# Hybrid decoder trunk on one core: the low halves of streamed weights and blocks formed by GpSimd instead of VectorE

## The chip, the core and the metric

The kernel runs on one core of a Trainium2 chip. The core has five engines with an instruction queue each: TensorE (PE, with its weight loads shown apart as PEld), VectorE (DVE), ScalarE (ACT), GpSimd (POOL) and SyncE (SP, which here only issues DMAs). An engine works through its queue in order and waits on semaphores. The metric is the time on the device in microseconds; the median of three runs before the change is 1358.11 us (1356.87 to 1358.42).

## What is computed

A decoder trunk of two layers over one sequence of 1024 positions with 1024 features, float32 in and out. Cut to what matters:

```python
def even_mixer(h, w_in, ...):                      # layer 0
    xa, ga, q, k, v, gb = split(h @ w_in)          # one projection, six parts
    ya = rg_lru(conv(xa)) * silu(ga)
    q, k = rms_norm(q, q_g), rms_norm(k, k_g)      # per head of 128
    yb = stick_breaking_attention(q, k, v) * silu(gb)
    return concatenate([ya, yb]) @ w_out

def odd_mixer(h, w_in, ...):                       # layer 1
    u, g = split(h @ w_in)
    y = gelu(s5_ssm(u))
    y = y * sigmoid(y @ glu_w + glu_b)
    return (y * silu(g)) @ w_out

for layer in range(2):
    h, gate = ada_modulate(x, c, ...)              # norm, scale, shift from c
    x = x + gate * mixer(h)
```

## The kernel before

Float32 products are made from two halves each: an operand x is split into a high half hi (x rounded to the fp32r format) and a low half lo = x - hi, and a product is hi*hi + hi*lo + lo*hi, three matmuls. Activations are split once and kept; weights are streamed from HBM and split as they come. The method `split` does it for a tensor that lies in SBUF: ACT casts to hi, DVE subtracts to lo (lines 72 and 75). The method `load_split` takes one of the two buffers of the pool `raw` (128 x 1024 floats), has SP load into it, and splits it.

Three things go through `load_split`:
- the weights of all projections (`w_raw`, `w_hi`, `w_lo`), 60 pieces of 128 x 1024: `w_fetch` keeps one piece ahead, with two buffers each for hi and lo. They serve the eight attention gates, the RG-LRU projections, the output projection of layer 0 (twice eight), the input projection of layer 1 (sixteen) and the GLU (eight).
- the q, k and v weights of heads 1 to 7 (`wqkv`), three chunks each, into a buffer that exists once, so that a chunk can be cast only when the last query block of the head before has been projected.
- the eight blocks of attention output (`yb`), written to HBM by the heads and loaded again for the output projection.

The two raw buffers are also used by the rows of the adaLN matrix (`ada_raw`), which DVE multiplies and sums in the heads (line 288, four rows a head), so all these loads stand in one line on SP, and each waits until the buffer two loads back is free.

The stages in order: a head part (norm of layer 0, to about 90 us), eight attention heads of about 67 us each (to 607), RG-LRU (to 790), the output projection in two halves (to 960), layer 1 with its S5 state space (to 1180), the GLU (to 1270) and the last projection. Within a head PE's order is written by hand: the gate's first matmuls, the transposes of the last query block's q and k (line 793), the rest of the gate, scores (lines 814 to 816), and then in turn qkv projections of eight query blocks for the next head (lines 767 to 769), transposes of the attention weights (line 832) and their products with v (lines 843 to 845). For each query block ACT squares q and k with a running sum (line 773), POOL turns the two sums into a factor (`pow_rstd`, lines 312 and 313), and DVE scales with it (line 776). The keep factors go through a scan on DVE (line 820), beta follows (lines 821, 822), PE transposes beta, and DVE forms the low half of the result (line 835).

POOL also issues the DMAs that write intermediate results to HBM: the tables of S5 (lines 689, 722, 729), the heads' output (962), the rotation tables (1215) that DVE makes in the output projection, x (1179), and in layer 1 the S5 inputs and outputs and the gates (1297, 1380, 1306). The order on DVE, ACT, POOL and SP is set by a scheduler that estimates when each instruction could run; only PE's order is the program's.

Of the kernel before, what the change touches and what calls it, by code (L numbers as in the profile page):

```python
# [9 lines left out]
F32 = mybir.dt.float32  # L10
# [4 lines left out]
ALU = mybir.AluOpType  # L15
# [39 lines left out]
class Trunk:  # L55
# [10 lines left out]
        return self.tc.alloc_tile_pool(name=name, bufs=bufs, side=side, reuse_waits="tile", **kw)  # L66


    def split(self, raw, hi, lo, hi_engine="act"):
        nc = self.nc  # L70
        if hi_engine == "act":
            nc.scalar.copy(hi, raw)  # L72
        else:
            nc.vector.tensor_copy(hi, raw)
        nc.vector.tensor_sub(lo, raw, hi.bitcast(F32))  # L75

    def load_split(self, src, hi, lo):
        raw = self.rp.tile([P, 1024], F32, name="w_raw", tag="raw")
        self.nc.sync.dma_start(raw, src)
        self.split(raw, hi, lo)  # L80
        return raw

    def w_next(self, ahead=1):
# [1548 lines left out]
```

## Time and profile before

| | before |
|---|---|
| median of three runs | 1358.11 us |
| the profiled execution, its own time | 1358.47 us |
| its span | 1356.7 us |
| TensorE busy | 1319.6 us |
| VectorE busy | 1058.5 us |
| ScalarE busy | 639.0 us |
| GpSimd busy | 148.8 us |
| mean granted clock of TensorE | 0.999 of full speed |

A busy PE is not always PE at its peak, since matmuls overlap: one of 512 columns shows 0.39 us, and they start 0.23 us apart. The span is what lies between the first and the last record; the time of the execution has some 2 us more around it. The chain that ended last is followed back from the last instruction, at each step to what released it.

### The profile page before, as it was taken

Reading aid. Unit: us, or ns where it says so; the run is one execution under the profiler, and the core shown is the slowest. Engines: PE = TensorE matmul, PEld = TensorE weight load, DVE = VectorE, ACT = ScalarE, POOL = GpSimd, SP = SyncE. Lnnn points to the kernel's source line nnn. Section 1 sums busy time; section 2 is a strip of 40 time slices with the busy share of each in tenths; the row PEclk is TensorE's granted clock in tenths of the full one; section 3 lists DMA queues with packets and bytes.
Section 4 is the critical chain, followed back from the end, with each engine's and each line's share of the span. In section 5 each row is a group of like instructions: output and inputs, shape, how many; then the busy total and the mean of one; then the engine's idle time right before and its main releaser. Section 6 shows DMA issues by size and latency. Waiting matters only on the chain.

```text
span 1356.7 us, 18988 instructions
## 1 busy us (share of the span) xinstructions
PE 1319.6 (97%) x7020; PEld 1136.4 (84%) x7020; DVE 1058.5 (78%) x2049; ACT 639.0 (47%) x1270; POOL 148.8 (11%) x239
## 2 busy tenths in 40 slices
PE   7999999999999999999999999999999999999998
PEld 3898889999989898888887878888888888888777
DVE  7949988878787878988899787866588669754784
ACT  6544454545454545354998722123364434633421
POOL 0012212222212121210000000000000000000000
PEclk9999999999999999999999999999999999999999
DMA  8442051413141314312211164332448789454331
GB/s 321 164 145 78 28 174 49 128 50 128 50 128 50 128 50 129 111 59 76 68 40 55 47 237 151 109 125 98 150 156 256 224 236 256 121 170 135 93 124 62
DMA packets 73212, 168.16 MB, mean 124 GB/s; under 512 B 9536, under 2 KB 35264, under 8 KB 73120
## 3 DMA queue, kind: packets, MB, share of 16 engines
q1 hardware_dynamic: 62112, 128.34, 30.9%
q0 software_dynamic: 11008, 38.62, 7.9%
q8 instruction: 55, 0.90, 0.3%
q14 instruction: 37, 0.30, 0.1%
HBM read 126.10 MB, written 40.83 MB: 123 GB/s over the span
## 4 chain that ended last, share of the span: by engine, by line
PE 60%; DVE 25%; ACT 5%; DMA 3%; issue 3%; POOL 2%; DVEq 0%; ACTq 0%; POOLq 0%
PE bank L120 6%; PE bank L123 6%; PE bank L122 6%; PE bank L125 6%; PE bank L121 6%; PE bank L124 5%; DVE keep L820 3%; PE bank L767 3%; PE bank L769 3%; PE bank L768 3%; DMA ada_raw<-ada 3%; DVE ada_raw L288 2%; PE bank L832 1%; DVE wt_lo L835 1%; DVE beta L822 1%
## 5 line engine op out<-in xcount | busy, mean ns | idle before, releaser
L767 PE MATMUL bank<-wqkv_hi,h_hi 128*128 128x384 f32 x512 | 173.6, 339 | 0.0
L769 PE MATMUL bank<-wqkv_hi,h_lo 128*128 128x384 f32 x512 | 172.4, 337 | 0.0
L768 PE MATMUL bank<-wqkv_lo,h_hi 128*128 128x384 f32 x512 | 172.4, 337 | 0.0
L72 ACT CAST w_hi<-w_raw 128x1024 fp32r<-128x1024 f32 x60 | 63.0, 1049 | 198.7 <-PE bank L123 142.2
L75 DVE TENSOR_TENSOR w_lo<-w_raw,w_hi 128x1024 fp32r<-128x1024 f32 x60 | 73.1, 1218 | 36.3 <-ACT w_hi L72 36.1
L768 PEld LDWEIGHTS bank<-wqkv_lo,h_hi 128*128 128x128 f32 x512 | 96.6, 189 | 0.4
L767 PEld LDWEIGHTS bank<-wqkv_hi,h_hi 128*128 128x128 f32 x512 | 96.6, 189 | 0.3
L769 PEld LDWEIGHTS bank<-wqkv_hi,h_lo 128*128 128x128 f32 x512 | 96.5, 189 | 0.0
L120 PE MATMUL bank<-h_hi,w_hi 128*128 128x512 f32 x224 | 89.3, 399 | 0.0
L122 PE MATMUL bank<-h_hi,w_hi 128*128 128x512 f32 x224 | 87.8, 392 | 0.7 <-DVE xc L1009 0.7
L776 DVE TENSOR_SCALAR nat<-bank,ss 128x128 f32<-128x128 f32 x128 | 39.1, 345 | 62.7 <-POOL ss L313 46.3
L124 PE MATMUL bank<-h_hi,w_lo 128*128 128x512 f32 x224 | 87.3, 390 | 0.4 <-DVE w_lo L75 0.4
L123 PE MATMUL bank<-h_lo,w_hi 128*128 128x512 f32 x224 | 87.7, 391 | 0.0
L125 PE MATMUL bank<-h_hi,w_lo 128*128 128x512 f32 x224 | 87.7, 391 | 0.0
L121 PE MATMUL bank<-h_lo,w_hi 128*128 128x512 f32 x224 | 87.3, 390 | 0.0
L820 DVE TENSOR_TENSOR_SCAN keep<-keep,after 128x1024 f32<-128x1024 f32 (+3 forms) x64 | 86.4, 1349 | 0.0
L312 POOL TENSOR_SCALAR ss<-ss 128x2 f32<-128x2 f32 x64 | 36.1, 564 | 306.9 <-ACT nat L773 306.3
L778 ACT COPY nat<-bank 128x128 f32<-128x128 f32 x64 | 17.0, 266 | 96.4 <-DVE nat L776 96.4
L773 ACT ACTIVATE nat<-bank 128x128 f32<-128x128 f32 x128 | 34.3, 276 | 58.6 <-PE bank L769 40.0
L817 ACT ACTIVATE keep<-bank 128x512 f32<-128x512 f32 (+2 forms) x96 | 48.5, 505 | 20.3 <-PE bank L816 18.8
L832 PE MATMUL bank<-ident,beta 128*128 128x128 f32 x288 | 43.5, 279 | 12.1 <-DVE wt_lo L835 8.9
L288 DVE SCALAR_TENSOR_TENSOR ada_raw<-ada_raw,cs 128x1024 f32<-128x1024 f32 x39 | 47.6, 1220 | 9.0 <-DMA ada_raw<-ada 8.9
(434 smaller groups left out, 3724.2 us busy)
## 6 DMA issues: line engine op xcount, KB each, us to landing
ada_raw<-ada SPq DMA_DIRECT2D x39, 512.0 KB, 4.2
w_raw<-wqkv SPq DMA_DIRECT2D x21, 512.0 KB, 3.6
w_raw<-wfm SPq DMA_DIRECT2D x20, 512.0 KB, 3.6
w_raw<-woe SPq DMA_DIRECT2D x16, 512.0 KB, 3.7
w_raw<-wod SPq DMA_DIRECT2D x16, 512.0 KB, 4.2
x<-xT SPq DMA_DIRECT2D x8, 512.0 KB, 7.1
cx_s<-ce POOLq DMA_DIRECT2D x16, 256.0 KB, 2.8
win_s<-wsb POOLq DMA_DIRECT2D x16, 256.0 KB, 3.3
```

What stands on the lines that cost most here:

```text
L75: nc.vector.tensor_sub(lo, raw, hi.bitcast(F32))
L120: nc.tensor.matmul(ps[0], wh[:, k, :], rh[k][:, h0], start=first, stop=False)
L121: nc.tensor.matmul(ps[0], wh[:, k, :], rl[k][:, h0], start=False, stop=False)
L122: nc.tensor.matmul(ps[1], wh[:, k, :], rh[k][:, h1], start=first, stop=False)
L123: nc.tensor.matmul(ps[1], wh[:, k, :], rl[k][:, h1], start=False, stop=False)
L124: nc.tensor.matmul(ps[0], wl[:, k, :], rh[k][:, h0], start=False, stop=last)
L125: nc.tensor.matmul(ps[1], wl[:, k, :], rh[k][:, h1], start=False, stop=last)
L288: v.scalar_tensor_tensor(raw, raw, 1.0, self.cs, op0=ALU.mult, op1=ALU.mult, accum_out=m)
L767: nc.tensor.matmul(ps[:, 0:384], hh[:, k, ts], wqh[:, ks], start=(k == 0), stop=False)
L768: nc.tensor.matmul(ps[:, 0:384], hh[:, k, ts], wql[:, ks], start=False, stop=False)
L769: nc.tensor.matmul(ps[:, 0:384], hl[:, k, ts], wqh[:, ks], start=False, stop=(k == KT - 1))
L820: v.tensor_tensor_scan(rev, rev, self.after[:, T - n:T][:, ::-1], 1.0, op0=ALU.mult, op1=ALU.max)
```

## The change

`load_split` no longer calls `split`: ACT casts to hi as before, and the subtraction is issued on GpSimd, as a `tensor_tensor` with the same operands. `split` loses a parameter that nobody used, and goes on subtracting on VectorE for everything that is split in place (activations, conv outputs, gates, y). Two lines fewer stand ahead of all other code, so a line of the changed kernel has a number lower by two from there on.

```diff
-    def split(self, raw, hi, lo, hi_engine="act"):
+    def split(self, raw, hi, lo):
+        self.nc.scalar.copy(hi, raw)
+        self.nc.vector.tensor_sub(lo, raw, hi.bitcast(F32))
+
+    def load_split(self, src, hi, lo):
         nc = self.nc
-        if hi_engine == "act":
-            nc.scalar.copy(hi, raw)
-        else:
-            nc.vector.tensor_copy(hi, raw)
-        nc.vector.tensor_sub(lo, raw, hi.bitcast(F32))
-
-    def load_split(self, src, hi, lo):
         raw = self.rp.tile([P, 1024], F32, name="w_raw", tag="raw")
-        self.nc.sync.dma_start(raw, src)
-        self.split(raw, hi, lo)
+        nc.sync.dma_start(raw, src)
+        nc.scalar.copy(hi, raw)
+        nc.gpsimd.tensor_tensor(lo, raw, hi.bitcast(F32), op=ALU.subtract)
         return raw
```

The scheduler places the moved instruction anew. On POOL at the end of a head (here the second), before the change:

```order
L312 TENSOR_SCALAR ss<-ss 128x2
L313 TENSOR_TENSOR ss<-ss,mh 128x2
L722 DMA win_s_1132<-wsb 128x512
L729 DMA rp_s_1148<-rpad 128x240
L962 DMA yb_s_607<-yb 128x1024
L689 DMA cx_s_1141<-ce 128x4x128
```

and now (lines 310, 311, 720, 727, 960 and 687 are 312, 313, 722, 729, 962 and 689 of before; line 78 is the moved subtraction):

```order
L78 TENSOR_TENSOR wqkv_lo<-w_raw,wqkv_hi 128x1024 x2
L310 TENSOR_SCALAR ss<-ss 128x2
L311 TENSOR_TENSOR ss<-ss,mh 128x2
L720 DMA win_s_1132<-wsb 128x512
L727 DMA rp_s_1148<-rpad 128x240
L960 DMA yb_s_607<-yb 128x1024
L78 TENSOR_TENSOR wqkv_lo<-w_raw,wqkv_hi 128x1024
L687 DMA cx_s_1141<-ce 128x4x128
L78 TENSOR_TENSOR w_lo<-w_raw,w_hi 128x1024
```

Two chunks of the next head's weights now stand ahead of the norm step of the head's last query block, the third behind three DMA issues, and the gate's weight behind a fourth.

On DVE at the same kind of place (here the fourth head's end), before:

```order
L799 SCALAR_TENSOR_TENSOR kt_lo<-bank_73,cols,kt_hi 128x256
L75 TENSOR_TENSOR wqkv_lo<-w_raw,wqkv_hi 128x1024 x2
L776 TENSOR_SCALAR nat<-bank_69,ss 128x128 x2
L726 SCALAR_TENSOR_TENSOR rpad<-eye_81,cols,rpad 64x16
L846 TENSOR_TENSOR yb<-bank_76,sgb 128x32x8
```

and now:

```order
L797 SCALAR_TENSOR_TENSOR kt_lo<-bank_73,cols,kt_hi 128x256
L670 COPY bd<-bb 64x8x16 x2
L681 TENSOR_TENSOR ce<-craw,pw 128x2x144
L684 TENSOR_TENSOR ce<-craw,pw 128x2x144
L724 SCALAR_TENSOR_TENSOR rpad<-eye_81,cols,rpad 64x16
L774 TENSOR_SCALAR nat<-bank_69,ss 128x128 x2
L844 TENSOR_TENSOR yb<-bank_76,sgb 128x32x8
```

The subtractions have left, and the first products of the S5 tables (`ce`) have moved up into their place. Further on in the same head the fourth ada row (line 288, now 286) has moved up from behind the second scan to the place between the first scan and its beta.

On POOL in the output projection, before, only the issues of rotation tables (`rot_s`) and x (`x_s`) stood behind the last head's output:

```order
L962 DMA yb_s_613<-yb 128x1024
L1215 DMA rot_s_7930<-rot 128x1024
L1215 DMA rot_s_7931<-rot 128x1024
L1215 DMA rot_s_7932<-rot 128x1024
L1215 DMA rot_s_7933<-rot 128x1024
L1215 DMA rot_s_7934<-rot 128x1024
```

and now, around the fifth to the seventh table:

```order
L78 TENSOR_TENSOR yb_lo<-w_raw,yb_hi 128x1024
L1213 DMA rot_s_7934<-rot 128x1024
L78 TENSOR_TENSOR w_lo<-w_raw,w_hi 128x1024
L78 TENSOR_TENSOR yb_lo<-w_raw,yb_hi 128x1024
L1213 DMA rot_s_7935<-rot 128x1024
L78 TENSOR_TENSOR w_lo<-w_raw,w_hi 128x1024
L1213 DMA rot_s_7936<-rot 128x1024
L78 TENSOR_TENSOR w_lo<-w_raw,w_hi 128x1024
```

The weights' and blocks' subtractions now alternate with the tables' issues, each of which waits until DVE has made its table.

## Rows read from the trace of the kernel before

**Rows 1.** The page: busy time of each engine; shares of the chain that ended last.

```profile
PE 1319.6 (97%) x7020; PEld 1136.4 (84%) x7020; DVE 1058.5 (78%) x2049; ACT 639.0 (47%) x1270; POOL 148.8 (11%) x239
...
PE 60%; DVE 25%; ACT 5%; DMA 3%; issue 3%; POOL 2%; DVEq 0%; ACTq 0%; POOLq 0%
```

**Rows 2.** Line 75: count, shortest/median/longest ns, first and last start, shapes.

```profile
L75 DVE TENSOR_TENSOR w_lo<-w_raw,w_hi x60: 1194/1218/1227, 83.0 to 1249.2; 128x1024 fp32r<-128x1024 f32 x60
L75 DVE TENSOR_TENSOR wqkv_lo<-w_raw,wqkv_hi x21: 1216/1219/1226, 111.0 to 523.8; 128x1024 fp32r<-128x1024 f32 x21
L75 DVE TENSOR_TENSOR yb_lo<-w_raw,yb_hi x8: 1212/1222/1226, 793.2 to 860.0; 128x1024 fp32r<-128x1024 f32 x8
```

**Rows 3.** POOL: memsets (busy us, mean ns), and lines 312 and 313 as above.

```profile
L265 POOL MEMSET ones<- 128x128 f32 x1 | 0.2, 204 | 0.3 <-POOLq L1622 0.3
...
L652 POOL MEMSET bd<- 128x256 f32 x1 | 0.3, 311 | 59.2 <-DVE wqkv_lo L75 59.2
...
L312 POOL TENSOR_SCALAR ss<-ss x64: 186/367/1662, 80.1 to 589.3; 128x2 f32<-128x2 f32 x64
...
L313 POOL TENSOR_TENSOR ss<-ss,mh x64: 688/691/4085, 80.3 to 589.5; 128x2 f32<-128x2 f32 x64
```

**Rows 4.** Timeline (start, length in us) at the end of the second head.

```profile
247.58 2.36 DVE L75 TENSOR_TENSOR wqkv_lo<-w_raw,wqkv_hi 128x1024 fp32r<-128x1024 f32 x2 [0.45 <-ACT wqkv_hi L72]
...
249.10 0.89 POOL L312 TENSOR_SCALAR ss<-ss 128x2 f32<-128x2 f32 x1 [5.43 <-ACT nat L773]
...
250.79 0.61 DVE L776 TENSOR_SCALAR nat<-bank,ss 128x128 f32<-128x128 f32 x2 [0.86 <-POOL ss L313]
...
252.59 0.60 PE L793 MATMUL bank<-ident,nat 128*128 128x128 f32 x4
```

**Rows 5.** Timeline in the first head: line 313 under products on DVE.

```profile
131.82 4.08 POOL L313 TENSOR_TENSOR ss<-ss,mh 128x2 f32<-128x2 f32 x1
...
134.66 0.68 DVE L641 TENSOR_TENSOR bb<-bb,t 128x512 f32<-128x512 f32 x1
```

**Rows 6.** Waits: who for whom, us in total, times, longest.

```profile
DVE nat L776 <- POOL ss L313: 46.3, 31, 10.0
...
PE bank L832 <- DVE wt_lo L835: 8.9, 8, 3.0
...
PE bank L793 <- DVE nat L776: 1.1, 1, 1.1
```

**Rows 7.** Timeline in the third head: DVE's steps and PE's transposes.

```profile
262.63 1.23 DVE L288 SCALAR_TENSOR_TENSOR ada_raw<-ada_raw,cs 128x1024 f32<-128x1024 f32 x1 [0.50 <-DMA ada_raw<-ada]
...
266.54 1.22 DVE L822 TENSOR_TENSOR beta<-beta,keep 128x1023 f32<-128x1023 f32 x1
...
267.98 1.04 PE L832 MATMUL bank<-ident,beta 128*128 128x128 f32 x8
...
272.76 1.21 DVE L75 TENSOR_TENSOR w_lo<-w_raw,w_hi 128x1024 fp32r<-128x1024 f32 x1
...
275.15 1.15 PE L832 MATMUL bank<-ident,beta 128*128 128x128 f32 x7 [0.93 <-DVE wt_lo L835]
```

**Rows 8.** Windows: length; PE, PEld, DVE, ACT, POOL busy; clock, DMA, GB/s.

```profile
607.00:790.00 183.00, 179.73 (x853) 148.20 (x852) 157.44 (x173) 139.57 (x177) 2.90 (x5) 1.00 0.21 67
...
960.00:1180.00 220.00, 220.00 (x1283) 184.58 (x1282) 169.09 (x202) 106.24 (x141) 15.31 (x23) 1.00 0.72 209
```

**Rows 9.** Timeline in the output projection: weight, rotation table, and use on PE.

```profile
854.37 1.22 DVE L75 TENSOR_TENSOR w_lo<-w_raw,w_hi 128x1024 fp32r<-128x1024 f32 x1
...
859.73 0.53 POOL L1215 DMA_DIRECT2D rot_s<-rot  x1 [15.24 <-DVE rot L1214]
...
860.22 0.39 PE L124 MATMUL bank<-ya,w_lo 128*128 128x512 f32 x1
```

**Rows 10.** Timeline in S5: the state on DVE and its use on PE.

```profile
1141.60 0.68 DVE L1350 TENSOR_TENSOR H<-m,m 64x508 f32<-64x508 f32 x1
...
1143.11 0.39 PE L1376 MATMUL bank<-H,cx 128*128 128x128 f32 x2
```

## Prediction

> **What bounds the kernel now.** I read the page first, then the stages, then the waits, then the timeline around each place where the moved instruction stands. The profiled execution took 1358.47 us, 1356.7 of it span; the median of the runs is 1358.11, so 0.4 us lie between what I count against and what is measured. TensorE is busy 1319.6 us [rows 1], which leaves 37.1 us that any change could win, some of it at the start and the end, where no weight is streamed. The reader is to see two things in rows 1: PE has 97% of the span, yet the chain that ended last gives 25% of its time to DVE. PE and DVE are thus close to each other in places. GpSimd is busy 11% only: it does the two small steps of the q/k norm for each query block (lines 312 and 313, 64 times) and issues DMAs.
>
> **What is removed from DVE.** 60 subtractions of 1.218 us, 21 of 1.219 and 8 of 1.222 [rows 2]: 73.1 + 25.6 + 9.8 = 108.5 us, a tenth of DVE's 1058.5. Nearly all of it lies under matmuls. It is worth only what PE waits for DVE.
>
> **What the same instruction costs on POOL.** No row shows POOL read two tensors of 1024 elements. A memset of 256 elements takes 311 ns and one of 128 takes 204 [rows 3]: 0.84 ns an element and about 0.1 us fixed, so one stream of 1024 is 0.95 us. The subtraction has two reads and a write. Side by side they take 0.95 us, the two reads in turn 1.8, all three in turn 2.7. I take 2.2, between the last two, and keep 0.95 to 2.7: 89 x 2.2 = 196 us on POOL, which has room, so what counts is who stands behind it. The Trainium skill (GPSIMD Engine Reference, 3.1) gives 4497 ns for a two-input add of 2048 elements, by which I estimate 2.25 us here; no run here shows it, and the sum would be 0.6 us higher.
>
> **Contention.** Line 312 takes 186 ns at best and 367 in the median, line 313 688 and up to 4085 [rows 3]. The long ones stand under DVE instructions with two SBUF inputs: at 249.10 line 312 took 0.89 us and ended at 249.99, when DVE's second subtraction (247.58 and 2.36 for two) had ended at 249.94 [rows 4]; at 131.82 line 313 took 4.08, and the last of six such products on DVE ended at 134.66 + 0.68 = 135.34 [rows 5]. So POOL waits for them, even for several in a row. The other direction, DVE waiting for a long read of POOL, no row shows: its price is between 0 and the whole 2.2 us.
>
> **The end of each head.** This is the first term. POOL's order now has the low halves of wqkv chunks 0 and 1 ahead of the norm step of the last query block. The first subtraction could start at 247.58 [rows 4]. Two of 2.2 us end at 251.98; lines 312 and 313 then take 0.19 + 0.08 + 0.69 and line 776 0.35 (0.61 for two), 1.3 in all: 253.3. PE took up the transposes of that block at 252.59, in order, with the gate matmuls behind them. It waits 0.8 us; nothing is lost up to (252.59 - 247.58 - 1.3) / 2 = 1.85 us a subtraction. For contention with the two products that DVE now has there I add 0.5 (line 312 lost 0.70 to one [rows 4]): 1.3 us, 0 to 2.7. Seven heads have this place. The first lies at the start of the first head, ahead of PE's longest wait for line 835, 3.0 us [rows 6], which three subtractions less on DVE (3.7 us) remove: there I let loss and gain cancel (-2 to +5). The other six: +7.8 us (0 to 16).
>
> **The two raw buffers.** All loads of a head (wqkv, four ada rows, the gate weight) go through two buffers in turn, and SP waits for the buffer. Chunk 2 is loaded when chunk 0 is subtracted, then ada row 1 when chunk 2 is, then row 3 after row 1. Chunk 2 now stands on POOL behind the norm step and three DMA issues. Before, DVE waited 0.50 us for ada row 2 at 262.63 and had beta ready at 266.54 + 1.22 = 267.76, when PE came at 267.98 [rows 7]: 0.2 us to spare. Chunk 2 comes 1 us later by each longer subtraction ahead of it and more when DVE's products keep POOL out; the new DVE order also puts ada row 3 before that beta, 1.2 us. Against it stand three subtractions less on DVE and a PE that is itself 1.3 us late. I take +0.8 a head, 0 to 2.1: six heads, +4.8 us (0 to 12.6).
>
> **The relief.** At 275.15 PE waits for the low half of the weights' transposes (line 835), which stood behind the gate weight's subtraction at 272.76 on DVE [rows 7]. All such waits are 8.9 us in eight places [rows 6], 5.9 without the 3.0 above. The subtraction leaves DVE, but now contends on POOL with the scan there and has the next norm step behind it, so I take half: -3.0 us (-5.9 to 0).
>
> **The other stages.** RG-LRU: PE idles 183.0 - 179.7 = 3.3 us between 607 and 790 while DVE is busy 157.4 [rows 8]. POOL has nothing else there, so the weight is ready sooner: -1 us (-3.3 to +4, the latter if a third of twelve longer subtractions reaches PE). Output projection: w_lo now stands on POOL behind the issue of the rotation tables, in order. Before, the fifth table was ready at 859.73, and DVE had made the weight at 854.37 that PE wanted at 860.22 [rows 9]. Were the tables as late as before, that weight would be ready at 859.73 + 0.54 + 2.2 = 862.5, 2.3 us late. DVE has two subtractions less for each table, 2.4 us, so the fifth can come up to 12 us sooner; I take +2 us (0 to 14, the upper end if DVE waits for POOL instead). S5: the state is ready at 1141.60 + 0.68 = 1142.28, PE wants it at 1143.11 [rows 10], 0.8 us of cover; a subtraction on POOL in the way of its chain costs 1.0 us more than DVE's own did: eight chains, +1.5 us (0 to +5). GLU and the last projection: nothing.
>
> **The sum.** 7.8 + 4.8 - 3.0 - 1.0 + 2.0 + 1.5 = +12.1 us on 1358.5: 1370.6 us.
>
> **The rivals.**
> *Relief wins.* If a subtraction on POOL stays under 1.85 us and finds its gaps, the ends of the heads cost nothing and DVE's 108.5 us count: -5.9 and -3.0 in the heads, -3.3 in RG-LRU, at most -12: 1347 to 1355. For it: a quarter of the chain is DVE. Against it: POOL's starts wait for DVE [rows 5], and after RG-LRU PE has no idle time to give back: it is busy 220.0 of 220 us from 960 to 1180 [rows 8]. 0.22.
> *The port decides.* DVE with two SBUF inputs waits out POOL's whole subtraction. Each of the 89 then takes 2.2 us from DVE and returns 1.2: 89 us more on an engine at 78%. With every head term at its upper end (16 + 12.6 + 5), no relief, +4, +10 and +5: +53, 1411; from half of it on I count this case: 1386 to 1411. For it: the lock shows in one direction [rows 5]. Against it: POOL gave way there, and DVE is idle for 22% of the span, where a subtraction finds the port free. 0.16. The Trainium skill (SBUF — State Buffer, Who interferes with whom) says that the two exclude each other for a whole instruction and whichever starts first blocks the other, which is this rival; the trace agrees for POOL's side and shows nothing of DVE's.
> *Hidden anyway.* Loss at the heads and relief cancel: 1355.8 to 1361.2. For it: 0.8 us at the end of a head is no more than the 0.93 that PE waits later in the same head [rows 7]. 0.16.
> That the change doesn't do what it says is excluded by the order: all 89 stand on POOL.
>
> **How the numbers follow.** The forecast (1361 to 1386) has 0.46. Slower by over 0.2%, which is 2.7 us and about what a measurement of this kernel tells from no change: 0.46 + 0.16 = 0.62; same 0.16; faster 0.22. Leaving out half of the fast case and half of the port's, the range is 1351 to 1396; within slower alone it is 1361 to 1396.
>
> **What would show it.** The subtraction's mean on POOL (2.2 us; over 3 speaks for the port). At each end of a head a wait of PE's transposes for line 776 (now one in all, of 1.1 us), and line 776's waits for POOL, now 46.3 us [rows 6], a good deal longer. DVE's mean per two-input form: unchanged in the forecast, longer if the port decides. In the output projection a wait of PE for w_lo. PE's waits for line 835 halved. I am wrong if the ends of the heads show no wait, or if the time is lost after 790.

## The result and the profile after

The changed kernel takes 1421.76 us (median of four runs, 1418.76 to 1423.43), the kernel before 1357.49 beside it: a ratio of 1.0471, 95% interval 1.0457 to 1.0485. It is 64 us slower; 1370.6 was forecast, in a range of 1351 to 1396. The direction was right and the size five times too small.

The profiled execution has a span of 1420.2 us (1356.7 before). Its page, busy time and the chain that ended last, against [rows 1]:

```profile
PE 1336.8 (94%) x7020; PEld 1144.2 (81%) x7020; DVE 1075.9 (76%) x1960; ACT 637.7 (45%) x1270; POOL 379.9 (27%) x328
...
PE 55%; DVE 22%; DMA 7%; issue 6%; POOL 5%; ACT 4%; SPq 0%; POOLq 0%; DVEq 0%; ACTq 0%
```

The line to stop at is DVE's. 108.5 us of subtractions have left it, and it is busy 17.4 us longer: what stayed takes 125.9 us more. (Neighbours on DVE overlap a little; added up instruction by instruction it is 116 us.) PE idles 83.4 us instead of 37.1 and is busy 17.2 us longer. The subtraction itself, by line (shortest, median and longest in ns; the eight `yb_lo` are alike), against [rows 2]:

```profile
L78 POOL TENSOR_TENSOR w_lo<-w_raw,w_hi x60: 2338/2406/4153, 84.3 to 1313.6; 128x1024 fp32r<-128x1024 f32 x60
L78 POOL TENSOR_TENSOR wqkv_lo<-w_raw,wqkv_hi x21: 2372/2407/4684, 111.7 to 555.2; 128x1024 fp32r<-128x1024 f32 x21
```

2.41 us free, near the 2.2 that I took. The Trainium skill (GPSIMD Engine Reference, 3.1), from which I estimated 2.25, is close too. The longest, 4.2 and 4.7, waited for DVE, as foreseen.

Which of DVE's instructions grew? Groups by form (total busy us, mean ns), before:

```profile
L835 DVE TENSOR_TENSOR wt_lo<-bank,wt_hi 128x512 fp32r<-128x512 f32 x48 | 32.0, 678 | 0.5 <-ACT wt_hi L834 0.5
L846 DVE TENSOR_TENSOR yb<-bank,sgb 128x256 f32<-128x256 f32 x32 | 19.9, 622 | 1.1 <-PE bank L845 0.7
L672 DVE COPY bd<-bb 64x128 f32<-64x128 f32 x16 | 3.6, 224 | 1.8 <-PE bank L713 1.7
L1078 DVE TENSOR_TENSOR ya<-gate,ya_slot 128x1024 f32<-128x1024 f32 x8 | 16.2, 2026 | 0.0
L820 DVE TENSOR_TENSOR_SCAN keep<-keep,after 128x896 f32<-128x896 f32 x8 | 16.1, 2015 | 0.0
L1482 DVE TENSOR_TENSOR x<-sgl,gsr 128x1024 f32<-128x1024 f32 x8 | 9.8, 1223 | 0.5 <-ACT sgl L1481 0.5
```

and after:

```profile
L833 DVE TENSOR_TENSOR wt_lo<-bank,wt_hi 128x512 fp32r<-128x512 f32 x48 | 32.0, 679 | 0.5 <-ACT wt_hi L832 0.5
L818 DVE TENSOR_TENSOR_SCAN keep<-keep,after 128x896 f32<-128x896 f32 x8 | 23.6, 2956 | 0.0
L670 DVE COPY bd<-bb 64x128 f32<-64x128 f32 x16 | 22.6, 1413 | 11.9 <-PE bank L711 11.7
L1076 DVE TENSOR_TENSOR ya<-gate,ya_slot 128x1024 f32<-128x1024 f32 x8 | 21.8, 2726 | 0.1
L844 DVE TENSOR_TENSOR yb<-bank,sgb 128x256 f32<-128x256 f32 x32 | 19.8, 619 | 0.9 <-PE bank L843 0.7
L1480 DVE TENSOR_TENSOR x<-sgl,gsr 128x1024 f32<-128x1024 f32 x8 | 19.3, 2407 | 5.6 <-ACT sgl L1479 5.3
```

The split is clean. Forms that take an input from PSUM (`bank`) have not changed: 678 and 679, 622 and 619 ns. Forms that read SBUF alone are up to twice as long, and the small copy `bd` six times. Over all forms, those with `bank` grew by 0.0 us in sum, and the 116 us lie in those that read SBUF alone. This is the rival "the port decides": DVE waits out POOL's whole subtraction. The Trainium skill (SBUF — State Buffer, Who interferes with whom) says so of a DVE instruction with two SBUF inputs against a GpSimd instruction that reads SBUF; the trace agrees, 2015 against 2956 ns for the scan.

Where PE waits now (us in total, times, longest), against [rows 6]:

```profile
PE bank L791 <- DVE nat L774: 12.6, 7, 5.1
PE bank L122 <- POOL w_lo L78: 9.7, 6, 2.6
PE bank L830 <- DVE beta L820: 8.3, 4, 3.0
...
PE bank L813 <- DVE kt_lo L797: 6.3, 7, 1.3
PE bank L830 <- DVE wt_lo L833: 5.5, 5, 1.4
PE bank L1051 <- DVE xcl L71: 3.6, 2, 2.9
```

Three places show how a wait comes about. RG-LRU, timeline (start, length), where POOL has nothing but the weight's subtraction:

```profile
737.90 2.28 DVE L1071 TENSOR_TENSOR_SCAN gate<-a,gate 128x1024 f32<-128x1024 f32 x1
...
738.60 3.73 POOL L78 TENSOR_TENSOR w_lo<-w_raw,w_hi 128x1024 fp32r<-128x1024 f32 x1 [17.50 <-ACT w_hi L77]
...
740.10 3.31 DVE L71 TENSOR_TENSOR xcl<-xc,xch 128x1024 fp32r<-128x1024 f32 x1
...
743.47 0.79 PE L1051 MATMUL bank<-xcl,gh 128*128 128x512 f32 x1 [2.88 <-DVE xcl L71]
```

POOL waits for the scan (to 740.18) and ends 2.15 us later, at 742.33; DVE's next instruction, of 1.21 us, waits for POOL and ends at 743.41; PE waits 2.88. The weight that was moved is not late at all: what is late is a product that stayed on DVE.

The output projection, where port and queue work together:

```profile
891.10 2.43 POOL L78 TENSOR_TENSOR yb_lo<-w_raw,yb_hi 128x1024 fp32r<-128x1024 f32 x1 [5.40 <-ACT yb_hi L77]
...
891.18 2.50 DVE L1212 TENSOR_TENSOR rot<-rot,rot 128x128 f32<-128x128 f32 x1
...
896.63 0.56 POOL L1213 DMA_DIRECT2D rot_s<-rot  x1 [3.10 <-DVE rot L1212]
897.21 2.35 POOL L78 TENSOR_TENSOR w_lo<-w_raw,w_hi 128x1024 fp32r<-128x1024 f32 x1
...
899.61 0.50 PE L122 MATMUL bank<-ya,w_lo 128*128 128x512 f32 x1 [2.59 <-POOL w_lo L78]
```

A step of the rotation table that takes 0.28 us takes 2.50 behind the subtraction. The table is later by that much, POOL stands idle until it may issue it, and the weight that PE wants stands behind the issue.

The end of the third head's work, the place that the forecast worked out:

```profile
258.40 4.73 POOL L78 TENSOR_TENSOR wqkv_lo<-w_raw,wqkv_hi 128x1024 fp32r<-128x1024 f32 x2 [3.94 <-ACT wqkv_hi L77]
...
259.58 3.64 DVE L670 COPY bd<-bb 64x128 f32<-64x128 f32 x2 [1.68 <-PE bank L711]
...
263.22 0.19 POOL L310 TENSOR_SCALAR ss<-ss 128x2 f32<-128x2 f32 x1
263.49 0.77 POOL L311 TENSOR_TENSOR ss<-ss,mh 128x2 f32<-128x2 f32 x1
...
264.79 0.81 PE L791 MATMUL bank<-ident,nat 128*128 128x128 f32 x4 [1.25 <-DVE nat L774]
```

On POOL the norm step stands behind two subtractions, and on DVE two copies of 0.22 us each take 3.64.

Last, the clock. Windows (length; PE, PEld, DVE, ACT, POOL busy; granted clock, DMA, GB/s) 1.2 us behind a wait of PE (2.29 us, to 284.37), and behind that:

```profile
285.60:289.00 3.40, 3.40 (x13) 3.40 (x12) 3.40 (x4) 1.00 (x3) 3.23 (x3) 0.50 0.51 140
289.00:292.40 3.40, 3.40 (x23) 3.37 (x22) 3.40 (x6) 1.53 (x5) 0.27 (x1) 1.00 0.15 63
```

For 3.4 us the granted clock is 0.50 (1.2 GHz instead of 2.4), and 13 matmuls fit where then 23 do. Before there was one such stretch (the last microseconds of the span left out), now there are eight, and each begins during a wait of PE or at most 1.2 us behind its end. At half of 3.4 us each, the seven new ones cost some 12 us by estimate, a fifth of the loss.

PE's 7020 matmuls stand in the same order in all the kernels here, so the delay of each against before can be read, and its growth by stage is what a stage lost. The stages are bounded by the times of before; the first row is the changed kernel, the others are the experiments below. The clock column is such an estimate for all of a kernel's stretches at half clock beyond the one of before; it is a part of the loss, not an addition to it.

| us lost by stage | to 92 | heads, to 607 | RG-LRU, to 790 | output proj., to 874 | to 960 | layer 1, to 1180 | GLU and last | of it clock, some | DVE's other work grew by | time against before |
|---|---|---|---|---|---|---|---|---|---|---|
| changed kernel | 1.3 | 31.1 | 11.2 | 13.7 | 0.0 | 6.9 | -0.7 | 11.9 | 125.9 | 1.0471 |
| add_read | 0.0 | 39.8 | 5.9 | 15.5 | 6.8 | 5.9 | -0.8 | 25.6 | 86.4 | 1.0542 |
| add_copy | 0.0 | 19.5 | 2.3 | 3.5 | 4.1 | 2.5 | 0.8 | 15.4 | 36.3 | 1.0269 |
| add_fill | 0.4 | 0.5 | -0.1 | 0.0 | 0.0 | 3.2 | -0.8 | 0 | 3.4 | 1.0045 |
| halves | 0.2 | 31.6 | 6.3 | 10.8 | 0.0 | 14.1 | -0.3 | 17.1 | 115.6 | 1.0461 |
| norm_dve | 0.8 | 25.2 | 10.2 | 12.0 | 0.0 | 5.3 | 0.9 | 11.9 | (it gained work) | 1.0403 |
| reorder | -0.1 | 40.0 | 7.8 | 0.9 | 7.1 | 7.1 | 1.1 | 27.3 | 135.9 | 1.0493 |
| gate_only | 0.6 | 8.2 | -1.0 | 0.0 | 0.0 | 0.0 | -0.7 | 6.8 | 14.5 | 1.0058 |
| lru_only | 0.8 | 1.0 | 8.0 | 2.7 | 0.0 | 0.0 | 0.8 | 6.8 | 17.7 | 1.0090 |
| glu_only | 1.7 | -1.6 | -0.7 | 0.0 | 0.0 | 0.0 | -0.5 | 1.7 | 14.4 | 1.0000 |

(DVE's growth is its busy time less 1058.5 us, with the moved subtractions taken off: 108.5 for 89 of them, 8.5 for 7, 13.4 for 11, 19.5 for 16. Stages and clock are from the one profiled execution of each kernel; the mean granted clock of all its runs says the same: 0.990 to 0.991 in the changed kernel, 0.977 to 0.980 in `reorder`, 0.995 to 1.000 before.)

### The profile page after: what moved, and what is told of

Its sections match the earlier page's. It is cut to its first block, busy times and chain, and to the rows that moved or that the text cites. A ratio compares the mean times of both kernels' runs of the same rounds, so it can differ in the third digit from the quotient of the medians.

```text
span 1420.2 us, 19043 instructions
## 1 busy us (share of the span) xinstructions
PE 1336.8 (94%) x7020; PEld 1144.2 (81%) x7020; DVE 1075.9 (76%) x1960; ACT 637.7 (45%) x1270; POOL 379.9 (27%) x328
## 4 chain that ended last, share of the span: by engine, by line
PE 55%; DVE 22%; DMA 7%; issue 6%; POOL 5%; ACT 4%; SPq 0%; POOLq 0%; DVEq 0%; ACTq 0%
PE bank L118 4%; PE bank L120 4%; PE bank L122 4%; PE bank L121 4%; PE bank L123 4%; PE bank L119 4%; PE bank L765 4%; PE bank L767 4%; PE bank L766 4%; DMA ada_raw<-ada 3%; DVE keep L818 2%; DVE ada_raw L286 2%; POOL w_lo L78 2%; PE bank L830 2%; PE bank L193 1%
## 5 line engine op out<-in xcount | busy, mean ns | idle before, releaser
L78 POOL TENSOR_TENSOR w_lo<-w_raw,w_hi 128x1024 fp32r<-128x1024 f32 x60 | 158.6, 2643 | 436.3 <-ACT w_hi L77 416.6
L818 DVE TENSOR_TENSOR_SCAN keep<-keep,after 128x1024 f32<-128x1024 f32 (+3 forms) x64 | 93.9, 1467 | 0.0
L774 DVE TENSOR_SCALAR nat<-bank,ss 128x128 f32<-128x128 f32 x128 | 39.1, 345 | 59.7 <-POOL ss L311 43.1
L310 POOL TENSOR_SCALAR ss<-ss 128x2 f32<-128x2 f32 x64 | 25.6, 400 | 186.1 <-ACT nat L771 184.2
L78 POOL TENSOR_TENSOR wqkv_lo<-w_raw,wqkv_hi 128x1024 fp32r<-128x1024 f32 x21 | 61.4, 2940 | 32.1 <-ACT wqkv_hi L77 28.9
L286 DVE SCALAR_TENSOR_TENSOR ada_raw<-ada_raw,cs 128x1024 f32<-128x1024 f32 x39 | 51.9, 1332 | 14.7 <-DMA ada_raw<-ada 13.0
L1334 DVE TENSOR_TENSOR m<-L,rot 128x1024 f32<-128x1024 f32 x32 | 42.4, 1367 | 23.5 <-DMA rot<-rot_s 17.9
```

What stands on the lines that cost most here:

```text
L78: nc.gpsimd.tensor_tensor(lo, raw, hi.bitcast(F32), op=ALU.subtract)
L286: v.scalar_tensor_tensor(raw, raw, 1.0, self.cs, op0=ALU.mult, op1=ALU.mult, accum_out=m)
L818: v.tensor_tensor_scan(rev, rev, self.after[:, T - n:T][:, ::-1], 1.0, op0=ALU.mult, op1=ALU.max)
```

## The experiments

Two theories were tested: the lock (DVE's instructions on SBUF wait out POOL's) and the queue (things stand behind a long instruction on POOL).

**A reading and a writing instruction on POOL, with every weight still made by DVE.** Behind each of the 89 subtractions of the kernel before, `add_read` and `add_fill` give POOL work on the used raw buffer that nobody needs; place and buffer are the same, the length is alike (1.9 us free, and 2.4). The two versions of the method `extra`, without its calls:

```diff
+    def extra(self, raw):                 # add_read
+        self.nc.gpsimd.tensor_tensor(raw, raw, raw, op=ALU.subtract)
...
+    def extra(self, raw):                 # add_fill
+        for n in (1024, 1024, 512):
+            self.nc.gpsimd.memset(raw[:, 0:n], 0.0)
```

> The kernel before, with VectorE still making every low half; behind each of the 89 subtractions GpSimd gets one more instruction, raw minus raw over the used raw buffer (two SBUF inputs, 1024 elements), whose result nobody needs. No weight waits for GpSimd, so of the change only its reading instruction is left (its place in GpSimd's queue and the raw buffer held longer included). Lock theory (VectorE instructions with SBUF inputs wait out a reading GpSimd instruction): VectorE's other forms grow by 80 to 120 us in sum, as in the changed kernel, those with a PSUM input do not grow, and the time rises by 20 to 50 us over before. Queue theory (the loss is work that stands behind the long instruction on GpSimd): VectorE's forms keep their means, and the time rises by 5 to 20 us, in the heads alone, where the norm step stands behind it.

> As the run with the added reading instruction, but GpSimd fills the used raw buffer instead: memsets of 1024, 1024 and 512 elements, by the rows of before 0.95 + 0.95 + 0.53 = 2.4 us together, as long as the subtraction of the changed kernel, in the same place, holding the same buffer, reading nothing. Lock theory: VectorE's forms keep their means, and the time rises by no more than 5 to 15 us, for the queue and the buffer. Queue theory: the same time as the run with the reading instruction, within 4 us.

Measured: 1432.47 us against 1361.75, ratios 1.0542 (1.0511 to 1.0572) and 1.0045 (1.0030 to 1.0061). Busy times of `add_read` and its instruction on POOL:

```profile
PE 1349.8 (94%) x7020; PEld 1152.5 (81%) x7020; DVE 1144.9 (80%) x2049; ACT 639.4 (45%) x1270; POOL 340.6 (24%) x328
...
L86 POOL TENSOR_TENSOR w_raw<-w_raw 128x1024 f32<-128x1024 f32 x89 | 197.5, 2219 | 406.3 <-DVE w_lo L75 215.7 <-issue 92.0 <-DVE wqkv_lo L75 53.7
```

and of `add_fill`:

```profile
PE 1320.4 (97%) x7020; PEld 1137.2 (84%) x7020; DVE 1061.9 (78%) x2049; ACT 638.1 (47%) x1270; POOL 362.9 (27%) x506
...
L87 POOL MEMSET w_raw<- 128x1024 f32 (+1 forms) x267 | 216.5, 815 | 394.5 <-DVE w_lo L75 317.3 <-DVE wqkv_lo L75 52.2 <-issue 10.3
```

POOL works about as long in both, 197.5 and 216.5 us, and holds the buffers alike. What reads costs 76 us, above the 20 to 50 expected of the lock, of which some 26 are the clock (table); what only writes costs 5, with no new stretch at half clock. So the loss needs no weight that is made late on POOL, and a place of this length in POOL's queue costs 5 us: that POOL reads SBUF while DVE does is enough. DVE's work grew by 86.4 and 3.4 us.

**One input instead of two.** `add_copy` multiplies the raw buffer by 1 in place.

```diff
+        self.nc.gpsimd.tensor_scalar(raw, raw, 1.0, 0.0, op0=ALU.mult, op1=ALU.add)
```

> As the run with the added reading instruction, but with one SBUF input: GpSimd multiplies the used raw buffer by 1 in place (1024 elements), behind each of VectorE's 89 subtractions. If any GpSimd instruction that reads SBUF shuts VectorE out for its length, VectorE's SBUF forms grow in proportion to that length (some 30 to 70 us if it takes 1 to 1.5 us) and the time rises by 15 to 45 us over before. If it takes two inputs on GpSimd, or if the queue is what costs, the time rises by 2 to 8 us, as with the fills.

It takes 1.06 us in the median, DVE's work grew by 36.3 us, and the time is 1392.84 (1.0269, 1.0248 to 1.0290), 36 us above before, in the upper half of what the lock allowed. One input is thus enough to shut DVE out, for a shorter time: the loss is about half that of `add_read`.

**A shorter hold.** `halves` makes each subtraction in two instructions of 512 elements.

```diff
-        nc.gpsimd.tensor_tensor(lo, raw, hi.bitcast(F32), op=ALU.subtract)
+        for h in range(2):
+            hs = slice(h * 512, (h + 1) * 512)
+            nc.gpsimd.tensor_tensor(lo[:, hs], raw[:, hs], hi[:, hs].bitcast(F32), op=ALU.subtract)
```

> The changed kernel with each subtraction on GpSimd in two instructions of 512 elements. Lock theory: a VectorE instruction waits out 1.25 us at most instead of 2.4, the sum of VectorE's growth (112 us) falls to 55 to 90, and the time falls by 10 to 25 us against the changed kernel. Queue theory, and the theory that the longer subtraction itself is the price: what stands behind the pair waits as long as before, and the time is within 4 us of the changed kernel or some us above it for the second instruction's fixed part.

1421.45 us (1.0461, 1.0430 to 1.0491): no change, as the queue theory said. The lock theory's inference was wrong here, not the lock: DVE's growth fell only from 125.9 to 115.6. The second half stands ready on POOL behind the first, so what DVE is spared per wait comes back as a second wait: 71 of its instructions in the changed kernel are over 0.15 us longer than the same form before, by 1.64 us in the mean, and here 108, by 0.99. RG-LRU got better (11.2 to 6.3 us), layer 1 worse (6.9 to 14.1, of which some 5 are the clock).

**The queue at the ends of the heads and behind the rotation tables.** `norm_dve` takes the norm step off POOL (with a product in place of the power, which this kernel leaves out), and `reorder` leaves it there but puts the order back. `LATE` names, for each rotation table, the subtraction that its issue is put behind.

```diff
-        nc.gpsimd.tensor_scalar(ss, ss, 1.0 / n, EPS, op0=ALU.mult, op1=ALU.add)      # norm_dve
-        nc.gpsimd.tensor_tensor(ss, ss, self.mh[:, 0:ss.shape[1]], op=ALU.pow)
+        nc.vector.tensor_scalar(ss, ss, 1.0 / n, EPS, op0=ALU.mult, op1=ALU.add)
+        nc.vector.tensor_tensor(ss, ss, self.mh[:, 0:ss.shape[1]], op=ALU.mult)
...
+        with self.tc.issue_after(self.normed.ins):                                    # reorder, load_qkv
+            self.load_split(self.I["wqkv"][hd][:, cs], self.wqh[:, cs], self.wql[:, cs])
...
+        with self.tc.issue_after(self.subs[self.sub0 + LATE[m]].ins):                 # reorder, rotations
+            nc.gpsimd.dma_start(self.rot_s[m], tb)
```

> The changed kernel with both steps of the q/k norm on VectorE instead of GpSimd; the power of the second step is left out and a multiplication of the same shape stands in its place, so that only its time is read. Queue theory: nothing PE waits for stands behind a subtraction at the ends of the heads any more, the transposes' waits for line 774 (12.6 us in 7) go, with the waits for the scores behind them (6.3 us in 7), and the heads lose 10 to 18 us less of their 31. Lock theory: the two steps now stand on VectorE, of which one has two SBUF inputs and waits out the subtraction instead; the ends of the heads keep half of their waits or more, and the time falls by under 8 us.

> The changed kernel with two pieces of GpSimd's order put back, all 89 subtractions staying there: at the ends of the heads the wqkv subtractions stand behind the norm step of the last query block, and in the output projection each rotation table's issue stands behind one or two more subtractions, so that no weight waits behind a table that is not yet made. Queue theory: the waits of the transposes for line 774 (12.6 us) and of the output projection for w_lo (9.7 us) go, and the time falls by 15 to 25 us against the changed kernel. Lock theory: VectorE still grows by 100 us or more and the waits come back elsewhere in the heads; the time falls by less than 10 us.

`norm_dve` takes 1413.68 us (1.0403, 1.0373 to 1.0434), 8 less (9 by the ratios), just past what the lock allowed. The heads lose 25.2 us instead of 31.1, less of a gain than the 10 to 18 of the queue theory, and the transposes still wait 9.1 us in 7 places. `reorder` takes 1423.07 (1.0493, 1.0466 to 1.0519), no less than the changed kernel, though what it aimed at is nearly gone: the transposes wait 0.8 us, and up to 874 the output projection loses 0.9 us instead of 13.7. So the queue was real there. But the loss came back: 8.9 us more in the heads, 7.1 in the second half of the output projection. The heads as a whole (windows as above), in the changed kernel and in `reorder`:

```profile
93.30:639.40 546.10, 505.67 (x3056) 468.21 (x3055) 453.65 (x1053) 248.44 (x765) 183.33 (x193) 0.99 0.26 83
...
91.90:646.90 555.00, 515.38 (x3056) 476.20 (x3055) 467.66 (x1054) 249.17 (x765) 168.77 (x193) 0.96 0.27 82
```

PE idles 40.4 us in the one and 39.6 in the other, against 17.2 before: the waits moved and are no more in sum. What is longer is PE's busy time, by 9.7 us, at a granted clock of 0.96 instead of 0.99: most heads now wait some 4 us at one place, for the scores, and the clock falls there. Over the whole kernel PE idles 75.2 us instead of 83.4 and is busy 1345.4 instead of 1336.8: what the order gained, the clock took back (some 27 us of it against 12). In the second half of the output projection it is the queue again: a weight's subtraction starts at 966.51 on POOL, right behind the issue of a table that waited 8.75 us, and PE waits 3.4 us for it. Timeline of `reorder` at the same end of a head:

```profile
271.08 3.26 DVE L701 TENSOR_TENSOR vv<-vv,s5t 128x256 f32<-128x256 f32 x1
...
271.70 2.35 POOL L79 TENSOR_TENSOR wqkv_lo<-w_raw,wqkv_hi 128x1024 fp32r<-128x1024 f32 x1
...
274.27 0.47 DVE L800 SCALAR_TENSOR_TENSOR qt_lo<-bank,cols,qt_hi 128x256 fp32r<-128x256 f32 x1
...
275.30 0.58 PE L815 MATMUL bank<-kt_hi,qt_hi 128*128 128x512 f32 x1 [4.10 <-ACT kt_hi L799]
```

A product of 0.42 us for a table of layer 1 (`vv`) takes 3.26 and ends only behind the subtraction, which ends at 274.05. Behind it in order stands `qt_lo`, which itself reads PSUM and would not have waited; ACT waits for that, and PE for ACT, 4.10 us.

**Parts of the change alone.** In `gate_only` 7 of the subtractions go to POOL, in `lru_only` 11, in `glu_only` 16 (second half of the output projection, and GLU).

```diff
+        if gps:
+            nc.gpsimd.tensor_tensor(lo, raw, hi.bitcast(F32), op=ALU.subtract)
+        else:
+            nc.vector.tensor_sub(lo, raw, hi.bitcast(F32))
...
+            raw = self.load_split(self.w_order[self.w_loaded], hi, lo, gps=0 < self.w_loaded < 8)                                # gate_only
+            raw = self.load_split(self.w_order[self.w_loaded], hi, lo, gps=9 <= self.w_loaded < 20)                              # lru_only
+            raw = self.load_split(self.w_order[self.w_loaded], hi, lo, gps=28 <= self.w_loaded < 36 or self.w_loaded >= 52)      # glu_only
```

> Of the 89 subtractions only the seven of the gate weights of heads 2 to 8 go to GpSimd, the others stay on VectorE: the place where the forecast saw relief (PE's waits for the low half of the attention weights, 8.9 us in 8 before). Relief: these waits fall by half and the time by 3 to 5 us against before. Lock theory: each subtraction shuts VectorE out of the scan chain for up to 2.4 us, seven of them, of which some reach PE; the time is 0 to 8 us above before.

> The kernel before with eleven of the 89 subtractions on GpSimd: those of the weights that RG-LRU fetches, a stage in which GpSimd has nothing else to do, so that nothing stands behind them on its queue and they stand behind nothing. Queue theory: the weight is ready in time or sooner and the time is within 3 us of before. Lock theory: VectorE's conv, scan and gate products wait them out, and the time rises by 5 to 12 us (the stage grew by 11.2 us in the changed kernel), PE waiting for the low half of a conv output.

> The kernel before with 16 of the 89 subtractions on GpSimd: those of the second half of the output projection and of the GLU, in which the changed kernel lost nothing. VectorE still waits them out (its SBUF forms there grow by 10 to 25 us), but PE has matmuls in hand that need nothing of VectorE, so the time is within 3 us of before; nor does it fall, though 16 x 1.22 = 19.5 us leave VectorE, since PE has no idle time there. A time over 5 us above before would say that the loss needs no work that waits on VectorE.

`gate_only` takes 1365.07 us (1.0058, 1.0041 to 1.0075). It is the place where relief was most likely, and it loses: the waits for the low half of the attention weights went up, from 8.9 us [rows 6] to 13.0, as DVE's other work grew by more (14.5) than the 8.5 that left it. But PE's idle time as a whole grew by only 1.6 us; it is busy 5.5 us longer, with 17.1 us at half clock instead of 3.4, so most of this loss is the clock. The waits:

```profile
PE bank L833 <- DVE wt_lo L836: 13.0, 7, 3.0
```

`lru_only` takes 1370.68 (1.0090, 1.0071 to 1.0109), slightly more than the 5 to 12 us of the lock theory, with almost nothing else in POOL's queue there. RG-LRU itself loses 8.0 us, the output projection 2.7; about half of the whole is the clock (some 6.8 us). PE waits for `xcl` as in the changed kernel, 2.9 us in two places (3.6 there). `glu_only` takes 1358.00 (1.0000, 0.9989 to 1.0010). DVE's other work grew by 14.4 us there too, and nothing came of it: PE had work in hand. Nor did it gain.

No version here beats the kernel before.

## Why the prediction was wrong

Term by term, with the steps of the prediction:

- *The price on POOL*, 2.2 us: right (2.41).
- *The end of each head*, +1.3 us in six heads and nothing in the first: right in mechanism and size for the six, where PE's transposes start 1.4 us late. In the first they waited 5.1, the end of the range there, and the relief that was to cancel it was small.
- *The two raw buffers*, +4.8: the mechanism was right, 8.3 us in four waits of line 830 for beta. In the third head chunk 2 was on POOL for 4.68 us (266.66 to 271.34), the next ada rows were issued only at 271.37, DVE took the row that stands ahead of beta at 281.86, and beta was ready at 284.23.
- *The relief*, -3.0: the number came, 8.9 us became 5.5, but the reason given is not shown: in `gate_only`, which moves just these weights, the same waits rose to 13.0. That PE is held up elsewhere in the heads of the changed kernel may be why they fell; no run tests it.
- *RG-LRU*, -1, and *S5*, +1.5: wrong in mechanism. They lost 11.2 and 6.9 us. "POOL has nothing else there, so the weight is ready sooner" counted only the weight; DVE's products were held up. In S5 a part of it lies on SP: a weight's load is issued at 1128.62, when the raw buffer comes free at the end of a subtraction (1128.60), with the loads for S5 behind it, and PE waits 2.5 us for them, to 1143.11. `add_fill` lost 3.2 us in this layer too, so up to half of the 6.9 may need no lock.
- *Output projection*, +2 of 0 to 14: the mechanism was right and the term mis-sized. I let the tables come sooner because DVE had less to do; they came later, since DVE waited for POOL, and the loss was 13.7.
- Two things had no term at all: the scores, which wait for `kt_lo` behind shut-out products on DVE (6.3 us in 7 places), and the clock (some 12 us). It falls at waits, and so it makes the terms above dearer.

The step that failed is thus the one under "Contention": for DVE waiting for POOL I wrote "no row shows: its price is between 0 and the whole 2.2 us", and then the sum took nearly 0. The runs put 125.9 us on DVE's other work by it, and in `add_read`, where nothing else is changed, 86.4 us and a loss of 76. A lock did show, in one direction [rows 5]; one that keeps a side out for a whole instruction can do so to the other when the order is reversed. The rival that said so had 0.16 and 1386 to 1411; its mechanism is the right one, though 1421.76 lies above its range too. Its arithmetic was off both ways. It put 89 us more on DVE, and 17.4 came, so the load was never the matter. But its upper end left out the scores and the clock, capped RG-LRU at 4, and took 10 for the output projection where the forecast itself went up to 14. The argument against it, that DVE is idle for 22% of the span, fails because a locked instruction stops all that stands behind it, `qt_lo` or the norm's scaling among them, which use no shared input.

Of the marks set beforehand, DVE's mean by form decided. The mean of the subtraction (2.64 for `w_lo`, 2.94 for `wqkv_lo`) stayed under my mark of 3 although the port decided, and line 776's wait for POOL did not grow (46.3 us before, 43.1 now): neither told the cases apart. The last mark was right, since a third of the loss lies after 790.

## What to carry to other kernels

An elementwise step with SBUF inputs that moves from VectorE to GpSimd hardly unloads VectorE: the two exclude each other, here 108.5 us went and 125.9 came back in other instructions. It cost nothing here only where no chain through VectorE is close to TensorE's next matmul, as in the second half of the output projection and the GLU, and there it gained nothing either. Before such a move, list what VectorE does at the same time by where its inputs lie, and what stands in order behind it; work for GpSimd that only writes was nearly free here (5 us). And when two versions take the same time, compare idle time and granted clock apart: `reorder` did take waits away from TensorE, and lost as much by the clock.

## What was not expected of the hardware

- A copy on DVE with a single SBUF input (line 672, 224 ns before) waits as well, 1413 ns in the mean in the changed kernel, and it is the one form that grew under the fills, by 4.3 us in 16. Why this form and not the norm's scaling is open; that one reads PSUM.
- In `reorder` a DVE instruction that began 0.6 us ahead of the subtraction (271.08 and 271.70) still ended only behind it. Why is open: the starts recorded on POOL are rough.
- All eight falls of TensorE to half clock stand at a wait, but a wait as long (2.5 us, to 1143.11) was followed by none, and `lru_only` shows three falls and `glu_only` one in stages whose subtractions were not moved, three of the four at a wait (1.0 us for scores, 2.1 us in the last projection) that before had no fall at it. Which wait has a fall behind it is open.
